# Retention's deviations taken on all partitions in the next phase, branch A's weights two chunks ahead, denser filling

## The chip, the cores and the metric

The kernel runs on one core of a Trainium2 chip. The metric is the device time of one execution in microseconds (us). The core's engines run side by side, each through its own queue in order: TensorE (PE) multiplies, VectorE (DVE), ScalarE (ACT) and GpSimd (POOL) work on elements, SyncE (SP) mostly issues DMAs. A wait at the head of a queue holds all that stands behind it there.

## The reference

One layer over 2048 tokens of width 1024, all in fp32 (cut):

```python
h = rms_norm(x, norm_gain[l])
proj = jnp.einsum('bsd,df->bsf', h, w_in[l])
q_a, k_a, v_a, g_a, q_r, k_r, v_r, g_r, m_a, m_r = split_columns(proj)
o_a = chunk_band_attention(q_a, k_a, v_a, rel_bias[l])           # 8 heads, chunks of 64, 8 chunks to the left
branch_a = jnp.einsum('bsf,fd->bsd', o_a * jax.nn.silu(g_a), w_out_attn[l])
o_r = retention_chunkwise(rotary(q_r), rotary(k_r), v_r, gn_gain[l])   # ends in:
#   o = (o - mean) * lax.rsqrt(var + GN_EPS), mean and var over the 128 values of a head
branch_r = jnp.einsum('bsf,fd->bsd', o_r * jax.nn.silu(g_r), w_out_ret[l])
mixed = jax.nn.sigmoid(m_a) * branch_a + jax.nn.sigmoid(m_r) * branch_r
x = rms_norm(x + jnp.einsum('bsd,de->bse', mixed, w_out[l]), final_gain)
```

## The kernel before

The tokens are worked in two halves of 1024, and each fp32 operand is split into a high and a low part (`wh`, `wl` for weights, the two tiles of `R[m]` for activations), so that a product of a 128x128 weight block takes three matmuls of 512 columns instead of one.

All dense products form one **stream**, made by `dense` (line 451): jobs p0 and g0 (projections and gates of the first half), p1 and g1 (second half), ba0 and ba1 (output product of branch A, the attention), br0 and br1 (branch B, the retention), out. A projection chunk is a Strassen scheme of seven products, gathered in PSUM banks x, y, v, z, w; a chunk of ba0 or ba1 is four plain products. A product is 12 matmuls, handed out in four **steps** of three. The counts are p0 up to step 392, g0 784, p1 1176, g1 1568, ba0 1632, ba1 1696, br1 1952, out 2208.

The phases are `proj0`, attention and retention of half 0, `proj1`, attention and retention of half 1, and `mrg`, the rest. Inside attention and retention, `fill(n)` lets the stream go on by n steps between the small matmuls of the phase, so that the other engines get time; `RET_FILLS` (line 60) is the number of steps that retention gives away twice per item (32 items per half: a pair of heads, a block of 256 tokens, one head of the pair). `later(n, fn)` (line 242) puts a piece of work off by n steps; `put` does so with a store. Up to the end of the second retention every engine gets its instructions in the order in which the code issues them; in `mrg` a scheduler may reorder ACT, DVE and POOL, while PE and SP stay in order.

`prime` (line 440) prepares the weights three products ahead: ACT casts `wh`, and DVE (or POOL) makes `wl` four steps later. The raw weights lie in a ring of three buffers (`RAWS`). In the stream, a chunk of a plain job is loaded over SP at the first product of the chunk ahead of it (line 474), so four products before its own start for ba0 and ba1.

In `retention` (line 1371) each item makes scores `sr` (PE), masks them with `dm` into `sm` (DVE), splits them into `sh` (ACT) and `sl` (POOL), and multiplies by the values into `o`; `oz` and `o` are copied and squared out of PSUM (ACT), `o2l` is the low part of the squares (POOL). Squares are summed over a head by matmuls with one-hot weights into the PSUM tile `ssq`, 32 rows (head and block) by 512 tokens. After the last item a chain of twelve DVE instructions on 32x512 tiles (`rt`, lines 1600 to 1615) makes the reciprocal roots, one instruction per step, and stores them to `rsscr`.

`finish_yr` (line 1071) reads them back as `rb`, spread over 128 partitions, and finishes one head and block of branch B (`yr` on DVE, then on POOL). While g0's last chunk runs, `reload` (line 799) puts the 28 activation tiles of half 1 into `R` (loads `r<-cs` on SP, ACT cast, DVE or POOL `r<-r`). In the second half `refill` does the same with `oas` (attention) and `yrs` (branch B).

Every instruction issued through the helper of line 140 carries that line in the profile, so rows are told apart by their tiles: `ps_g_z` is bank z of a gates job, `c_g` and `u_g` are the sums taken from such banks, `t_p` the Strassen sums of weights, `raw_ba` a raw chunk of branch A.

## Time and profile before

| | us |
|---|---|
| runs of the kernel before | 1987.76 median of 3 (1986.89 to 1991.05) |
| the profiled execution | 1993.2 |
| its span, first to last instruction | 1991.4 |
| PE busy in the span | 1926.9 |
| DVE busy | 1353.9 |
| ACT busy | 911.1 |
| POOL busy | 898.8 |

The profile is of one execution, in which the span plus 1.8 us around it makes its time. Its views name each instruction by engine, line, operation and tiles, and give an engine's idle time before it with what ended that. "PEclk" is the TensorE clock that was granted, as a share of full speed. A matmul's end is modelled, so what a wait costs PE is seen best from start to start.

### The profile page before, as it was taken

Reading aid. Unit: us, or ns where it says so; the run is one execution under the profiler, and the core shown is the slowest. Engines: PE = TensorE matmul, PEld = TensorE weight load, DVE = VectorE, ACT = ScalarE, POOL = GpSimd, SP = SyncE. Lnnn points to the kernel's source line nnn. Section 1 sums busy time; section 2 is a strip of 40 time slices with the busy share of each in tenths; the row PEclk is TensorE's granted clock in tenths of the full one; section 3 lists DMA queues with packets and bytes.
Section 4 is the critical chain, followed back from the end, with each engine's and each line's share of the span. In section 5 each row is a group of like instructions: output and inputs, shape, how many; then the busy total and the mean of one; then the engine's idle time right before and its main releaser. Section 6 shows DMA issues by size and latency. Waiting matters only on the chain.

```text
span 1991.4 us, 30303 instructions
## 1 busy us (share of the span) xinstructions
PE 1926.9 (97%) x9712; PEld 1604.3 (81%) x9712; DVE 1353.9 (68%) x2585; ACT 911.1 (46%) x1835; POOL 898.8 (45%) x735
## 2 busy tenths in 40 slices
PE   6899999999999999999999999999999999999998
PEld 4777778888888877778787888888888878888886
DVE  7887878677766658888887677765566655544554
ACT  6454454566654545443333555554455221222332
POOL 2343544555546665544544444454675114422222
PEclk9999999999999999999999999999999999999999
DMA  4576695756549987676675645554989999976564
GB/s 148 162 258 198 217 309 197 211 153 181 159 135 276 276 248 258 192 242 195 193 247 177 185 148 177 155 147 141 281 268 294 319 334 338 326 251 213 187 200 138
DMA packets 335054, 434.85 MB, mean 218 GB/s; under 512 B 30040, under 2 KB 194544, under 8 KB 334896
## 3 DMA queue, kind: packets, MB, share of 16 engines
q1 hardware_dynamic: 277744, 377.07, 59.6%
q10 hardware_dynamic: 57152, 55.85, 9.3%
q8 instruction: 78, 1.28, 0.3%
q14 instruction: 80, 0.66, 0.1%
HBM read 288.21 MB, written 144.60 MB: 217 GB/s over the span
## 4 chain that ended last, share of the span: by engine, by line
PE 50%; DVE 7%; DMA 4%; issue 3%; ACT 1%; POOL 1%; SPq 0%; DVEq 0%; POOLq 0%; ACTq 0%
PE ps_g_z L140 4%; PE ps_g_x L140 3%; PE ps_p_z L140 3%; PE po L140 2%; PE ps_p_x L140 2%; PE wide L140 2%; PE o L140 2%; PE ps_g_v L140 2%; PE ps_g_y L140 2%; PE ps_g_w L140 2%; PE tp L140 1%; PE ps_p_w L140 1%; PE ps_p_y L140 1%; DMA raw_ba<-in_w_out_attn_dram 1%; PE ps_p_v L140 1%
## 5 line engine op out<-in xcount | busy, mean ns | idle before, releaser
L140 POOL TENSOR_SCALAR pr<-pr,rsum 128x640 f32<-128x640 f32 (+4 forms) x128 | 96.5, 754 | 225.4 <-DVE ptl L140 105.4
L140 PE MATMUL ps_g_z<-r,wh_g 128*128 128x512 f32 x448 | 144.0, 403 | 4.2 <-DVE c_g L140 4.2
L140 PE MATMUL ps_p_z<-r,wh_p 128*128 128x512 f32 x448 | 141.5, 397 | 5.4 <-DVE c_p L140 2.8
L140 PE MATMUL ps_p_x<-r,wh_p 128*128 128x512 f32 x448 | 142.0, 398 | 1.4 <-ACT u_p L140 1.4
L140 PE MATMUL ps_g_x<-r,wh_g 128*128 128x512 f32 x448 | 142.5, 399 | 0.7 <-ACT u_g L140 0.7
L140 DVE CUSTOM_DVE_ANT_0 pr<-wide,bt 128x640 f32<-128x640 f32 (+4 forms) x128 | 94.3, 737 | 71.2 <-PE wide L140 63.8
L140 POOL TENSOR_TENSOR t_p<-raw_p,t_p 128x512 f32<-128x512 f32 x50 | 74.8, 1497 | 146.9 <-DVE wl_p L140 134.1
L140 ACT ACTIVATE pr<-pr,mn 128x640 f32<-128x640 f32 (+4 forms) x128 | 98.0, 766 | 85.0 <-DVE mn L140 85.0
L140 DVE TENSOR_TENSOR ptl<-tp,pth 128x384 fp32r<-128x384 f32 x168 | 95.9, 573 | 40.9 <-ACT pth L140 40.5
L140 ACT CAST pth<-tp 128x384 fp32r<-128x384 f32 x168 | 84.8, 516 | 70.1 <-PE tp L140 66.1
L140 POOL TENSOR_TENSOR sl<-sm,sh 128x512 fp32r<-128x512 f32 x64 | 88.0, 1376 | 61.5 <-ACT sh L140 25.5
L140 DVE TENSOR_TENSOR wl_p<-t_p,wh_p 128x512 fp32r<-128x512 f32 x112 | 105.1, 939 | 2.0 <-ACT wh_p L140 2.0
L1167 POOL TENSOR_TENSOR fg<-xr,fg 128x512 f32<-128x512 f32 x32 | 44.4, 1387 | 128.3 <-DVE xr L1161 100.5
L140 DVE TENSOR_TENSOR sm<-sr,dm 128x512 f32<-128x512 f32 x64 | 44.1, 689 | 82.7 <-DMA dm<-in_dmask_dram 35.2
L140 PEld LDWEIGHTS ps_p_z<-r,wh_p 128*128 128x128 f32 x448 | 81.7, 188 | 22.9 <-issue 5.5
L140 PEld LDWEIGHTS ps_p_x<-r,wh_p 128*128 128x128 f32 x448 | 83.7, 190 | 19.9 <-ACT u_p L140 2.2
L140 PE MATMUL wide<-ka,qa 128*128 128x512 f32 (+2 forms) x448 | 94.5, 327 | 2.3 <-DVE mn L140 2.3
L1125 POOL TENSOR_TENSOR gr<-gr,ta 128x512 f32<-128x512 f32 x32 | 47.7, 1492 | 105.0 <-DVE gr L1124 89.8
L140 POOL TENSOR_TENSOR wl_g<-t_g,wh_g 128x512 fp32r<-128x512 f32 x56 | 75.2, 1342 | 40.5 <-ACT wh_g L140 31.4
L140 PEld LDWEIGHTS tp<-ident,pr 128*128 128x128 f32 x560 | 71.2, 140 | 27.2 <-POOL pr L140 2.2
L140 PE MATMUL po<-pth,va 128*128 128x256 f32 x336 | 93.0, 297 | 0.0
L140 ACT CAST wh_p<-t_p 128x512 fp32r<-128x512 f32 x112 | 69.2, 619 | 49.5 <-PE ps_p_z L140 22.1
(1187 smaller groups left out, 5969.2 us busy)
## 6 DMA issues: line engine op xcount, KB each, us to landing
raw_g<-in_w_in_dram ACTq DMA_DIRECT2D x56, 512.0 KB, 5.4
raw_p<-in_w_in_dram ACTq DMA_DIRECT2D x50, 512.0 KB, 6.1
qa<-qas SPq DMA_DIRECT2D x128, 128.0 KB, 3.0
qr<-qrs SPq DMA_DIRECT2D x128, 128.0 KB, 4.2
vr<-vrs SPq DMA_DIRECT2D x64, 256.0 KB, 5.6
ka<-kas SPq DMA_DIRECT2D x40, 256.0 KB, 3.6
va<-vas SPq DMA_DIRECT2D x40, 256.0 KB, 3.0
kds<-kdt_k SPq DMA_DIRECT2D x32, 256.0 KB, 4.5
```

What stands on the lines that cost most here:

```text
L140: return tc.keep_in_program_order(op(*a, **k))
L1125: pool.tensor_tensor(g, g, ta, ALU.add)
L1167: pool.tensor_tensor(fg, xr, fg, ALU.mult)
```

## The change

Three things, in the code:

- `RET_FILLS` goes from (1.9, 2.2) to (2.0, 2.3).
- At the end of `retention` one ACT instruction scales `ssq` into `var` and a store takes it to a new scratch, `sqscr`. The chain runs in a new function, `deviations`, which loads those numbers as 128 partitions by 128 columns, adds the epsilon, takes the roots in twelve DVE instructions of 128x128 (one per step) and stores them to `rsscr`. It is called 6 steps into the projection of half 1 for half 0 and 24 steps into `mrg` for half 1. The eight `finish_yr` of half 0 start at 38 and come every 42 steps, where they started at 10 and came every 44.
- `dense` loads a chunk of ba0 and ba1 seven products before its own start instead of four.

In steps: retention of half 0 ended at 772 and now ends at 769, that of half 1 at 1600 and now at 1597; the last item ends at step 757 instead of 750, and at 1585 instead of 1578.

```diff
-RET_FILLS = (1.9, 2.2)
+RET_FILLS = (2.0, 2.3)
...
+    sqscr = [D(f"sqs_{s}", [32, B]) for s in range(2)]
...
+    def firsts_of(seq):
+
+        seen = set()
+        for at, (_, ch, _n) in enumerate(seq):
+            if ch not in seen:
+                seen.add(ch)
+                yield at, ch
...
+        short = {begins_plain - 7: ch for begins_plain, ch in firsts_of(seq) if ch.job.kh == 1}
...
+            if at in short and short[at].raw is None:
+                short[at].load()
...
-        y, tmp, hv, var = (E(f"rt{n}")[0:32] for n in range(4))
+        var = E("var")[0:32]
+        later(1, lambda: act.activation(var, ssq, AF.Copy, scale=1.0 / DV))
+        put(3, sqscr[s], var)
+        fill(3)
+
+    def deviations(s):
+
+        t = E(f"dev_{s}", shape=(P, 4, P))
+        v, y, tmp = (t[:, n] for n in range(3))
+        wide_ = lambda d: d.rearrange("r (q c) -> (r q) c", c=P)
+        dma(v, wide_(sqscr[s]))
         chain = [
-            lambda: dve.tensor_scalar(var, ssq, 1.0 / DV, GN_EPS, ALU.mult, ALU.add),
-            lambda: dve.tensor_scalar(tmp.bitcast(I32), var.bitcast(I32), 1, None, ALU.logical_shift_right),
+            lambda: dve.tensor_scalar(v, v, GN_EPS, None, ALU.add),
+            lambda: dve.tensor_scalar(tmp.bitcast(I32), v.bitcast(I32), 1, None, ALU.logical_shift_right),
...
-                lambda: dve.scalar_tensor_tensor(tmp, y, -0.5, var, ALU.mult, ALU.mult),
+                lambda: dve.scalar_tensor_tensor(tmp, y, -0.5, v, ALU.mult, ALU.mult),
...
-        chain.append(lambda: dma(rsscr[s], y))
         for n, fn in enumerate(chain):
-            later(1 + n, fn)
-        fill(len(chain))
+            later(9 + n, fn)
+        later(9 + len(chain) + 2, lambda: dma(wide_(rsscr[s]), y))
...
+    later(6, lambda: deviations(0))
     for h in range(HEADS):
-        later(10 + 44 * h, lambda h=h: finish_yr(h, 0, None, 18))
+        later(38 + 42 * h, lambda h=h: finish_yr(h, 0, None, 18))
...
+    later(24, lambda: deviations(1))
```

DVE at the end of the first retention, **before** (`rt` is the chain; `wl`, `u2`, `c22` belong to the gates' chunks 12 and 13, `r01` is a refilled activation tile):

```order
L140 TENSOR_TENSOR wl_g0_13_1_8977<-t2_g0_13_8809,wh_g0_13_1_8976 128x512
L140 TENSOR_SCALAR rt3_9015<-ssq_6950 32x512
L140 TENSOR_SCALAR rt1_9013<-rt3_9015 32x512
L140 TENSOR_SCALAR rt0_9012<-rt1_9013 32x512
L140 SCALAR_TENSOR_TENSOR rt1_9013<-rt0_9012,rt3_9015 32x512
L140 TENSOR_TENSOR rt1_9013<-rt1_9013,rt0_9012 32x512
L140 SCALAR_TENSOR_TENSOR rt0_9012<-rt1_9013,rt0_9012 32x512
L140 TENSOR_TENSOR wl_g0_13_4_9032<-t1_g0_13_8807,wh_g0_13_4_9031 128x512
```

and **now**, from the same `wl` on:

```order
L140 TENSOR_TENSOR wl_g0_13_1_8956<-t2_g0_13_8745,wh_g0_13_1_8955 128x512
L140 TENSOR_TENSOR wl_g0_13_4_9024<-t1_g0_13_8743,wh_g0_13_4_9023 128x512
L140 TENSOR_TENSOR u2_g0_13_9014<-ps_g0_13_y_9053,u2_g0_13_9014 128x512
L140 TENSOR_TENSOR r01_82<-r01_82,r00_81 128x512
L140 TENSOR_TENSOR u3_g0_13_9117<-ps_g0_13_v_9085,u2_g0_13_9014 128x512
L140 TENSOR_TENSOR r01_82<-r01_82,r00_81 128x512
L140 TENSOR_TENSOR wl_g0_13_6_9081<-raw_g0_13_1_8551,wh_g0_13_6_9080 128x512
L140 TENSOR_TENSOR c22_g0_13_9144<-ps_g0_13_z_9129,u3_g0_13_9117 128x512
```

All twelve instructions of the chain are gone from there, also the six that stood between the second `wl` and `c22`.

DVE early in the projection of half 1, **before** (`l_qa`, `l_ka` are low parts of queries and keys, `wl_p1` low weights of its first two chunks, `r31`, `r51` refilled tiles):

```order
L140 SCALAR_TENSOR_TENSOR l_qa_2_0_9269<-ps_p1_0_x_9227,h_qa_2_0_9268 128x512
L140 TENSOR_TENSOR r51_92<-r51_92,r50_91 128x512 x2
L140 TENSOR_TENSOR wl_p1_1_1_9275<-t2_p1_1_9225,wh_p1_1_1_9274 128x512
L140 TENSOR_TENSOR r51_92<-r51_92,r50_91 128x512
L140 TENSOR_TENSOR wl_p1_0_2_9307<-t3_p1_0_9251,wh_p1_0_2_9306 128x512
L140 TENSOR_TENSOR l_ka_2_0_9326<-ps_p1_1_x_9279,h_ka_2_0_9325 128x512
L140 TENSOR_TENSOR r31_88<-r31_88,r30_87 128x512
```

and **now**:

```order
L140 SCALAR_TENSOR_TENSOR l_qa_2_0_9259<-ps_p1_0_x_9215,h_qa_2_0_9258 128x512
L140 TENSOR_TENSOR r51_92<-r51_92,r50_91 128x512 x2
L140 TENSOR_TENSOR wl_p1_1_1_9265<-t2_p1_1_9213,wh_p1_1_1_9264 128x512
L140 TENSOR_SCALAR dev_0_9244<-dev_0_9244 128x128 x2
L140 TENSOR_TENSOR r51_92<-r51_92,r50_91 128x512
L140 TENSOR_SCALAR dev_0_9244<-dev_0_9244 128x128
L140 TENSOR_TENSOR wl_p1_0_2_9291<-t3_p1_0_9239,wh_p1_0_2_9290 128x512
L140 SCALAR_TENSOR_TENSOR dev_0_9244<-dev_0_9244 128x128
L140 TENSOR_TENSOR l_ka_2_0_9312<-ps_p1_1_x_9269,h_ka_2_0_9311 128x512
L140 TENSOR_TENSOR r31_88<-r31_88,r30_87 128x512
L140 TENSOR_TENSOR dev_0_9244<-dev_0_9244 128x128
L140 SCALAR_TENSOR_TENSOR dev_0_9244<-dev_0_9244 128x128
```

The chain, now `dev`, is spread one by one between the refills and the low weights; its other six instructions follow before `u3` of the first chunk, and the `yr` instruction that stood there has moved later.

SP in branch A's second job, **before** (`tas` stores and `ga` loads go with one product each, `yr`, `yv`, `rb` belong to `finish_yr`):

```order
L140 DMA tas_5_1_419<-ga_5_1_18043 128x512
L140 DMA ga_7_0_18122<-mas_7_0_362 128x512
...
L140 DMA rb_3_1_18185<-rss_0_439 128x512
L140 DMA tas_7_0_426<-ga_7_0_18122 128x512
L140 DMA raw_ba1_1_0_18195<-in_w_out_attn_dram 128x4x256
L140 DMA ga_0_3_18197<-mas_0_3_337 128x512
```

and **now**:

```order
L140 DMA tas_5_1_419<-ga_5_1_18042 128x512
L140 DMA dev_1_18115<-sqs_1_440 128x128
L140 DMA raw_ba1_1_0_18117<-in_w_out_attn_dram 128x4x256
L140 DMA ga_7_0_18122<-mas_7_0_362 128x512
L140 DMA tas_6_0_422<-ga_6_0_18064 128x512
```

The load of a raw chunk stands three `tas` stores, that is three products, earlier. In the tail of the second retention the same move puts `raw_ba0_1`, which stood behind the last values `vr_3_7`, directly ahead of `kd_3_6` and `vr_3_6`. At the end of the first retention the store of the roots (`rss`), which stood ahead of the weight loads of p1's second chunk and of the last 16 `r<-cs` loads, gives way to the store of `var` four loads further forward.

## Rows read from the trace of the kernel before

**Rows 1.** The page's busy time, share of the span and instructions of each engine.

```profile
PE 1926.9 (97%) x9712; PEld 1604.3 (81%) x9712; DVE 1353.9 (68%) x2585; ACT 911.1 (46%) x1835; POOL 898.8 (45%) x735
```

**Rows 2.** Windows: stretch, length; busy PE, PEld, DVE, ACT, POOL (count); PEclk; DMA share, GB/s.

```profile
573.00:762.00 189.00, 181.75 (x1030) 155.62 (x1029) 111.41 (x198) 92.43 (x175) 113.35 (x87) 0.99 0.78 236
1395.00:1557.00 162.00, 160.17 (x929) 139.47 (x929) 99.44 (x168) 86.58 (x160) 94.79 (x71) 1.00 0.92 284
1557.00:1640.00 83.00, 80.77 (x348) 64.41 (x347) 52.87 (x84) 20.65 (x36) 10.31 (x8) 1.00 0.94 327
...
774.00:784.00 10.00, 8.09 (x31) 6.24 (x30) 9.17 (x16) 4.33 (x8) 2.82 (x1) 0.85 0.63 189
784.00:800.00 16.00, 14.65 (x62) 11.46 (x61) 16.00 (x16) 11.10 (x22) 11.88 (x9) 0.99 1.04 380
```

**Rows 3.** PE's waits in 573 to 762 us: who waited for whom, us, times, longest.

```profile
PE ps_g_z L140 <- DVE c_g L140: 2.3, 1, 2.3
PE o L140 <- ACT o L140: 1.7, 3, 0.9
```

**Rows 4.** Groups of the chain on DVE, 760 to 780 us: busy us, mean ns.

```profile
L140 DVE SCALAR_TENSOR_TENSOR rt<-rt,rt 32x512 f32<-32x512 f32 x6 | 7.1, 1189 | 0.1
L140 DVE TENSOR_TENSOR rt<-rt,rt 32x512 f32<-32x512 f32 x3 | 3.0, 1007 | 0.1
L140 DVE TENSOR_SCALAR rt<-rt 32x512 int32<-32x512 int32 x2 | 1.8, 906 | 0.1
L140 DVE TENSOR_SCALAR rt<-ssq 32x512 f32<-32x512 f32 x1 | 0.7, 678 | 1.2 <-PE ssq L140 1.2
```

**Rows 5.** Timelines of DVE, then PE, after the chain: start, us, what, [idle before].

```profile
778.74 0.67 DVE L140 TENSOR_TENSOR c_g<-ps_g_z,u_g 128x512 f32<-128x512 f32 x1
...
779.56 0.70 PE L140 MATMUL ps_g_z<-r,wh_g 128*128 128x512 f32 x2 [1.91 <-DVE c_g L140]
```

**Rows 6.** Timeline of SP at the same place: start, us, DMA issued.

```profile
776.43 0.33 SPq L140 DMA_DIRECT2D rss<-rt  x1
...
779.54 7.32 SPq L140 DMA_DIRECT2D r<-cs  x12
```

**Rows 7.** Groups of all DVE work: the one that is nearest to 128x128.

```profile
L140 DVE SCALAR_TENSOR_TENSOR state<-state,kv 64x128 f32<-64x128 f32 x48 | 11.4, 274 | 16.8 <-PE kv L140 14.7 <-DMA mas<-g 2.1
```

**Rows 8.** Timelines of POOL, DVE and PE (in this order) early in proj1.

```profile
801.09 1.74 POOL L140 TENSOR_TENSOR t_p<-raw_p,t_p 128x512 f32<-128x512 f32 x1
...
807.54 1.30 POOL L140 TENSOR_TENSOR yr<-yr,rb 128x512 f32<-128x512 f32 x1 [1.29 <-DVE yr L140]
...
801.60 1.78 DVE L140 TENSOR_TENSOR r<-r,r 128x512 fp32r<-128x512 f32 x1
803.30 0.68 DVE L140 TENSOR_TENSOR u_p<-ps_p_y,u_p 128x512 f32<-128x512 f32 x1
...
806.72 0.74 DVE L140 SCALAR_TENSOR_TENSOR yr<-yr,gn,yv 128x512 f32<-128x512 f32 x1
...
814.53 0.50 PE L140 MATMUL ps_p_w<-r,wl_p 128*128 128x512 f32 x1 [0.38 <-DVE wl_p L140]
818.53 0.50 PE L140 MATMUL ps_p_w<-r,wl_p 128*128 128x512 f32 x1 [0.96 <-DVE wl_p L140]
```

**Rows 9.** Branch A: PE's first and last wait of three, SP's load, `raw_ba`'s landing times.

```profile
1599.36 0.74 PE L140 MATMUL ps_ba_(0, 0)_18298<-r,wh_ba_(0, 0)_18218 128*128 128x512 f32 x2 [1.01 <-ACT wh_ba_(0, 0)_18218 L296]
...
1623.73 0.73 PE L140 MATMUL ps_ba_(0, 0)_18490<-r,wh_ba_(0, 0)_18414 128*128 128x512 f32 x2 [0.57 <-ACT wh_ba_(0, 0)_18414 L296]
...
1591.32 0.39 SPq L140 DMA_DIRECT2D raw_ba<-in_w_out_attn_dram  x1
...
DMA to landing us min/median/max: 3.9/5.4/7.3
```

**Rows 10.** Second retention: one of PE's waits, 1395 to 1557 us; a window.

```profile
PE kv L140 <- DMA vr<-vrs: 0.7, 2, 0.5
...
1520.00:1530.00 10.00, 10.00 (x60) 8.78 (x60) 8.18 (x15) 7.38 (x14) 5.41 (x4) 1.00 1.03 337
```

## The prediction

> **What bounds the kernel now.** I read the shares of busy time first: PE is busy for 1926.9 us, 97% of the span, the other engines for 68% at most [rows 1]. The matmuls are the same in number and size after the change, so it can gain only where PE stands still or runs at the lower clock. The views to read are therefore the table of windows, for what PE lacks in each stage, and then the waits and timelines inside the stages that the change touches.
>
> Between 573 and 762 us (retention of half 0) PE is busy 181.75 of 189.00 us, so it idles 7.2 us; its mean granted clock of 0.99 costs another 1% of 189, 1.9 us. Between 1395 and 1557 us (most of the second retention) it idles 1.8 us at full clock [rows 2]. The two stages do the same work, but the first gives 1.9 steps to the stream at each place and the second 2.2. What PE waits for in the first is spread: `c_g`, a sum on DVE, once for 2.3 us, and `o`, which ACT has to copy out of PSUM, 1.7 us in three waits [rows 3].
>
> Right behind the first retention, between 774 and 784 us, PE idles 1.9 us and the granted clock is 0.85 [rows 2]. The timelines name the cause: product 6 of the last gates chunk waits 1.91 us for `c_g`, which DVE starts at 778.74 [rows 5], just behind the chain of roots. That chain takes DVE 7.1 + 3.0 + 1.8 + 0.7 = 12.6 us [rows 4]. SP stood in the same place: it issues the store of the roots at 776.43 and gets to the next twelve loads of `r<-cs` from 779.54 on [rows 6].
>
> In branch A, between 1557 and 1640 us, PE idles 83.00 - 80.77 = 2.2 us [rows 2], in three waits, each for the cast of a raw chunk (1.01 us the first, 0.57 the last). SP issued the first of those chunks at 1591.32 for a product that began at 1599.36, and such a load takes 3.9 to 7.3 us to land [rows 9].
>
> **The change part by part.** One step of the stream is 3 matmuls. In branch A 348 matmuls take 80.77 us [rows 2], 0.232 us each, so a step is 0.70 us and a product (12 matmuls) 2.8 us.
>
> *The chain leaves the end of the first retention.* DVE gets 12.6 us back there, and in its order nothing of the chain is left ahead of `c_g`. The bank's product 4 then has the whole of product 5, 2.8 us, as cover for a sum of 0.67 us [rows 5]. So I take the wait as gone: 1.9 us, and the lower clock behind it: (1 - 0.85) x 10 + (1 - 0.99) x 16 = 1.7 us [rows 2]. Together **-3.6 us**; no less than 0 and, with the waits named next also gone, 1.3 us more. ACT takes one instruction more, nothing to speak of at 911.1 us of 1991 [rows 1]. SP no longer stands until 776.43, so the refills of half 1 come earlier, which hides in the same gain.
>
> *The chain comes back in the projection of half 1.* By the order it stands among refills and low weights, from step 799 to 810, which in the trace of before is 795 to 805 us. There DVE has no time to spare: it is busy for all 16.00 us from 784 to 800 [rows 2], and soon after PE waits for `wl_p`, 0.38 and 0.96 us [rows 8]. The nearest row for one new instruction is 0.274 us, 64 partitions by 128 columns [rows 7]; twelve make 3.3 us. Against that `yr` of `finish_yr` leaves the stretch: 0.74 us on DVE, and 1.30 us of POOL [rows 8] of which DVE may wait most. Net 3.3 - 0.74 - 1.1 = 1.5 us of DVE time. Half of the chain comes before 800 us, where DVE is now ahead instead of behind, so I take half: **+0.7 us**. The lower bound is 0, the upper one follows from the next sentences.
>
> A `r<-r` (two operands in SBUF) takes 1.78 us when it starts inside a POOL instruction that runs from 801.09 for 1.74 us, and `u_p`, with one operand in PSUM, 0.68 us [rows 8]; the chain itself shows it too, with means of 1.19 and 1.01 us for instructions of which the first, from PSUM, took 0.68 [rows 4]. So a new instruction on SBUF may cost 1.78 - 0.68 = 1.1 us more whenever it meets POOL, however few columns it has: 12 x 1.1 + 1.5 = 14.7 us is the upper bound. The Trainium skill, in SBUF — State Buffer, section "SBUF: two separate sides", states this as a rule: VectorE and GpSimd share a port pair under an exclusive lock, held "for the full instruction". By that rule cutting 512 columns to 128 saves nothing of the wait, and the trace agrees as far as the 1.78 us shows. It speaks against this change and is the third rival below.
>
> I stay near the lower end because POOL runs no more instructions there than before, and nearly all of them hold a DVE instruction already; more DVE instructions don't make more POOL instructions to wait for.
>
> *The new DMAs.* The load of `dev` is issued 9 steps, 6.3 us, ahead of the chain; landing takes 3.9 to 7.3 us for far larger loads [rows 9], so it is hidden. The store stands on SP two steps behind the chain, and behind it wait stores of queries and keys and the loads of `finish_yr`, which nobody needs for tens of steps: 0, at worst 1 us. The roots are first needed at step 822.
>
> *The second chain.* It leaves the tail of the second retention and returns in branch A. From 1557 on PE waits for nothing but raw chunks, and DVE is busy 52.87 of 83.00 us, POOL 10.31 [rows 2]. Nothing on either side: 0.
>
> *Denser filling.* The steps are only moved, so each 0.1 buys slack alone: 0.1 x 0.70 us between any two small products. If the first retention at 1.9 lacks 7.2 + 1.9 = 9.1 us and the second at 2.2 lacks 1.8, the slope is 2.4 us for each 0.1. I take **-2.4 us** for the first. It may get all that the second has (-7.3); and since the stream's chunks slide against retention's items, a wait like the longest may fall in anew: 2.3 us and the 1.7 us of lower clock, +4.0. For the second I take 0 (bounds -1.8 and +1).
>
> *Branch A's weights.* Three products earlier is 8.4 us earlier; the three loads were late by 1 us at most [rows 9]. All 2.2 us go, and the slow first matmuls behind each wait (0.74 us for two, against 2 x 0.232) with them, about 0.16 x 3: **-2.7 us**, bounds -3 and 0. What becomes late next is nothing that waits today: three waits are all that the stretch has. But the second chunk of branch A now goes out directly ahead of the values of two of retention's last items, where the transfers run at 337 GB/s with a DMA share of 1.03 and PE already waits 0.7 us for `vr` [rows 10]. 512 KB at that rate are 1.6 us of delay, and denser filling gives back some: **+0.7 us**, bounds 0 and 1.6.
>
> The sum: -3.6 + 0.7 - 2.4 - 2.7 + 0.7 = **-7.3 us**. The profiled execution took 1993.2 us, span and surroundings, so it would take 1985.9. It lies 5.4 us over the median of its kernel's runs, 1987.76; the difference carried over gives **1980.5 us**.
>
> **The rivals.**
>
> *The waits of retention only slide.* The first retention gets no better but a wait like its longest more: +4.0 instead of -2.4, so -7.3 + 6.4 = -0.9 us, 1986.9: no change. For it: the waits have several causes [rows 3], and the stream is moved by only 7 steps in 140. Against it: the second retention, with more filling, has almost none.
>
> *Branch A's loads don't land earlier.* SP keeps order, and transfers are busy for 0.94 of the time [rows 2]. Then 2.7 us are missing: 1983.1. Against it: the order puts the load three `tas` stores forward, each of which waits for a product.
>
> *The chain meets POOL (slower).* In the projection of half 1, from 795 to 805 us, every one of the twelve waits for a POOL instruction, DVE falls 14.7 us behind, and PE waits for `wl_p` that long: -7.3 - 0.7 + 14.7 = +6.7 us, 1994.5. It decides from the point where 1.5 + 1.1 x n is over 8.0, that is from 6 of the 12 on. Against it: a POOL instruction takes 1.74 us there [rows 8], so ten us hold six at the most, and those already hold others. The skill's SBUF page, named above, would have this come out by its lock.
>
> *Everything clears.* The first retention does as the second (-7.3 in place of -2.4), and the `wl_p` waits go because DVE enters the projection without arrears (-1.3 and the +0.7): -7.3 - 4.9 - 2.0 = -14.2, 1973.6.
>
> **How the numbers follow.** The forecast has 0.55, the sliding waits 0.20, the late loads 0.08, POOL 0.07, everything clear 0.10. 0.2% of 1987.76 is 4.0 us, about what a measurement of this kernel can tell from no change: faster means below 1983.8. The forecast's spread of some 4 us either way puts 0.50 of its 0.55 there; with 0.05 of the late loads, 0.10 of the clear case and 0.02 of the sliding one that is 0.67. Slower is 0.06 from POOL and 0.01 from sliding waits, 0.07. The rest, 0.26, is no change. The range goes from 1973 to 1988: it holds the sliding case and the edge of the clear one, and leaves out POOL's.
>
> **What would show it.** Right: no wait for `c_g` behind the first retention and a clock of 1.00 there; no wait for `wh_ba`; PE's idle time in the first retention at some 5 us; waits for `wl_p` early in the projection no longer than 2 us. Wrong: `dev` rows of over 1 us each; a wait for `vr` of over 2 us at the end of the second retention; new waits of over 2 us with a clock near 0.5 in the first.

## The result, and the profile after

| | median of runs | runs |
|---|---|---|
| before, in the same session | 1987.11 us | 21 |
| changed kernel | 1992.53 us | 21 |
| ratio, changed to before | 1.0027, 95% interval 1.0019 to 1.0035 | |
| changed kernel again, in a later session (e12) | 1989.32 us against 1986.87; 1.0020, 1.0004 to 1.0036 | 11 and 27 |

By the two ratios the change costs 4 to 5 us; the medians differ by 5.4 and 2.5 us. The forecast was 1980.5, so it is 12 us too low and has the wrong sign. A few executions in the experiments were slow ones of over 2100 us, which the ratios leave out and the medians do not (e6's stands 0.8 us higher for it), so the readings go by the ratios.

The profiled execution of the changed kernel took 1999.27 us, 6.7 over its median. PE's line of the page, which answers to [rows 1]:

```profile
PE 1928.5 (97%) x9712; PEld 1608.2 (81%) x9712; DVE 1337.6 (67%) x2585; ACT 909.5 (46%) x1837; POOL 890.1 (45%) x735
```

The windows of the changed kernel that answer to [rows 2] (stretch, length; busy PE, PEld, DVE, ACT, POOL with counts; PE's granted clock; DMA share, GB/s):

```profile
573.00:762.00 189.00, 185.23 (x1062) 159.79 (x1061) 111.41 (x201) 95.62 (x182) 118.13 (x91) 1.00 0.82 247
...
774.00:784.00 10.00, 8.61 (x37) 6.43 (x37) 10.00 (x9) 7.31 (x14) 8.14 (x6) 1.00 1.05 394
...
1395.00:1557.00 162.00, 156.19 (x892) 134.92 (x891) 94.55 (x159) 81.39 (x153) 89.84 (x68) 0.99 0.89 274
1557.00:1640.00 83.00, 80.45 (x354) 66.09 (x353) 49.42 (x83) 22.44 (x40) 11.89 (x9) 0.98 0.96 332
```

PE's idle time in the first retention fell from 7.2 to 3.8 us, and the wait for `c_g` behind it is gone, as forecast. But the second retention, which idled 1.8 us, now idles 5.8, and branch A idles 2.5 us against 2.2. Both kernels were profiled once more, the kernel before as e11 and the changed kernel as e12, and much of this doesn't repeat. The kernel before, unchanged, idles 3.7 us in the same window of its second profile:

```profile
573.00:762.00 189.00, 185.32 (x1059) 159.16 (x1057) 117.79 (x206) 95.88 (x182) 118.16 (x90) 1.00 0.82 246
```

So the 3.8 us are no gain that can be put down to the change. In the other two windows e11 idles 2.4 and 1.4 us, e12 3.8 and 0.2.

In both profiles of the changed kernel PE no longer waits for a raw chunk in branch A [rows 9]. In the first one it waits for an epilogue on DVE, `ga`, instead; in e12 that wait is 0.2 us. The waits of PE from 1557 to 1640 us in the first profile (who for whom, us, times, longest), and DVE's timeline there (start, us, what, idle time before it and its releaser):

```profile
PE ps_ba_(1, 1)_18383 L140 <- DVE ga L1119: 2.6, 1, 2.6
```

```profile
1608.94 0.75 DVE L1092 SCALAR_TENSOR_TENSOR yr<-yr,gn,yv 128x512 f32<-128x512 f32 x1 [0.96 <-DMA yv<-urs]
1611.74 0.69 DVE L1102 TENSOR_TENSOR r<-yr,r 128x512 fp32r<-128x512 f32 x1 [2.05 <-ACT r L1101]
...
1613.55 0.68 DVE L1119 SCALAR_TENSOR_TENSOR ga<-ga,ps_ba_(1, 1)_18280 128x512 f32<-128x512 f32 x1
```

DVE takes its instructions in order. It stands 0.96 us for a load of `finish_yr` and 2.05 us for ACT's copy in the same helper, and the `ga` that would free PE's bank is queued behind both.

The larger losses lie in the projection of half 1, where the forecast had +0.7 us. The chain there, by groups on DVE from 784 to 803 us (busy us, mean ns), in the place of [rows 4]:

```profile
L140 DVE SCALAR_TENSOR_TENSOR dev<-dev 128x128 f32<-128x128 f32 x6 | 4.2, 693 | 0.1
L140 DVE TENSOR_TENSOR dev<-dev 128x128 f32<-128x128 f32 x3 | 3.0, 996 | 0.0
L140 DVE TENSOR_SCALAR dev<-dev 128x128 int32<-128x128 int32 x2 | 0.4, 224 | 0.0
L140 DVE TENSOR_SCALAR dev<-dev 128x128 f32<-128x128 f32 x1 | 0.2, 217 | 0.0
```

These are 7.8 us, against 12 x 0.274 = 3.3 us by [rows 7]. The timelines of DVE, POOL and PE at this place show why (`dev` rows of DVE, the POOL rows that run beside them, PE's next wait):

```profile
790.23 1.38 DVE L140 TENSOR_TENSOR dev<-dev 128x128 f32<-128x128 f32 x1
791.64 1.27 DVE L140 SCALAR_TENSOR_TENSOR dev<-dev 128x128 f32<-128x128 f32 x1
...
794.74 0.28 DVE L140 TENSOR_TENSOR dev<-dev 128x128 f32<-128x128 f32 x1
...
798.74 1.33 DVE L140 TENSOR_TENSOR dev<-dev 128x128 f32<-128x128 f32 x1
800.00 1.75 DVE L140 TENSOR_TENSOR wl_p<-t_p,wh_p 128x512 fp32r<-128x512 f32 x1
...
789.72 1.74 POOL L140 TENSOR_TENSOR t_p<-raw_p,t_p 128x512 f32<-128x512 f32 x1
791.42 1.34 POOL L140 TENSOR_TENSOR t_p<-b_p,t_p 128x512 f32<-128x512 f32 x1
792.72 1.34 POOL L140 TENSOR_TENSOR r<-r,r 128x512 fp32r<-128x512 f32 x1
795.52 1.45 POOL L140 TENSOR_TENSOR r<-r,r 128x512 fp32r<-128x512 f32 x1 [1.46 <-ACT r L140]
...
798.34 1.58 POOL L140 TENSOR_TENSOR t_p<-raw_p,t_p 128x512 f32<-128x512 f32 x1
...
801.80 0.55 PE L140 MATMUL ps_p_z<-r,wl_p 128*128 128x512 f32 x1 [3.92 <-DVE wl_p L140]
```

The `dev` of 790.23 starts inside POOL's `t_p`, which runs to 791.46, and ends at 791.61. The one of 791.64 ends at 792.91, behind a POOL instruction that runs to 792.76; the one of 798.74 at 800.07, behind one to 799.92. Each ends 0.15 us after POOL. The one of 794.74 falls in POOL's gap (794.06 to 795.52) and takes 0.28. Five of the twelve were held; the two that are not shown took 0.78 and 1.27 us and also ended 0.15 us after POOL. One that started 0.02 us behind a POOL instruction, at 795.54, was not held (0.28 us). `wl_p` comes behind them, and PE waits 3.92 us for it; in the kernel before it waited 0.38 and 0.96 us for other `wl_p`, two and six microseconds further into the stage [rows 8].

The second chain, in branch A, has the same twelve instructions with the same operands in SBUF, and no POOL instruction but one of 0.02 us runs beside it: there each takes 0.22 to 0.29 us, in both profiles. So it is the place that makes the chain slow, not the instructions.

Later in the same projection PE waits 1.78 us for `u_p`, a wait that the trace of before doesn't have. DVE, then POOL, then PE, in the changed kernel:

```profile
851.87 0.74 DVE L140 SCALAR_TENSOR_TENSOR yr<-yr,gn,yv 128x512 f32<-128x512 f32 x1
852.53 1.78 DVE L140 TENSOR_TENSOR xk<-xk,t_k 128x512 f32<-128x512 f32 x1
854.23 1.78 DVE L140 TENSOR_TENSOR u_p<-u_p,cs_k 128x512 f32<-128x512 f32 x1
856.05 1.63 DVE L140 TENSOR_TENSOR u_p<-u_p,t_k 128x512 f32<-128x512 f32 x1
...
852.03 1.73 POOL L140 TENSOR_TENSOR t_p<-raw_p,raw_p 128x512 f32<-128x512 f32 x1 [2.43 <-DVE wl_p L140]
853.72 1.74 POOL L140 TENSOR_TENSOR yr<-yr,rb 128x512 f32<-128x512 f32 x1
...
857.74 0.33 PE L140 MATMUL trkr_k<-ident,u_p 128*128 128x128 f32 x1 [1.78 <-DVE u_p L140]
```

The same two instructions on DVE in the kernel before:

```profile
858.89 0.68 DVE L140 TENSOR_TENSOR xk<-xk,t_k 128x512 f32<-128x512 f32 x1
859.50 1.78 DVE L140 TENSOR_TENSOR u_p<-u_p,cs_k 128x512 f32<-128x512 f32 x1
```

`u_p` is as slow there as in the changed kernel; what is new stands ahead of it. `yr` of the later `finish_yr` takes 0.66 us from start to start, and `xk`, which started 0.16 us before POOL's `t_p` (859.05) and took 0.68, now starts 0.50 us behind it and takes 1.78. That is 0.66 + 1.10 = 1.76 us, the wait of PE, whose transposes of `xk` and `u_p` come next. The POOL half of the same `yr` then runs beside `u_p`, where the kernel before has another POOL instruction.

The same stages in all profiles, from the first small product of a retention or the first product of a projection to the next such mark, read from PE's timelines. "First 14" and "rest" are the projection of half 1 up to the start of its fourteenth product after the first, and from there to its last; "ret 1 to B" goes from the second retention's first product to branch B's.

| kernel | ret 0 | first 14 | rest | ret 1 to B |
|---|---|---|---|---|
| before | 184.8 | 42.9 | 248.4 | 247.6 |
| before, again (e11) | 176.8 | 43.1 | 248.3 | 248.4 |
| changed | 173.8 | 46.3 | 253.6 | 254.8 |
| changed, again (e12) | 172.2 | 47.2 | 251.2 | 246.9 |
| e1: filling 2.0, 2.2 | 176.1 | 45.5 | 248.3 | 248.0 |
| e2: filling 1.9, 2.3 | 176.9 | 43.0 | 248.4 | 252.2 |
| e3: early loads | 179.7 | 43.1 | 248.3 | 244.6 |
| e4: `finish_yr` later | 184.0 | 41.0 | 252.6 | 249.1 |
| e5: chain and `finish_yr` | 178.7 | 47.1 | 252.6 | 249.9 |
| e6: changed, filling 2.0, 2.2 | 175.0 | 47.1 | 251.1 | 244.4 |
| e7: changed, no early loads | 173.0 | 46.4 | 253.8 | 248.9 |
| e8: changed, `y` in PSUM | 171.5 | 42.8 | 252.4 | 247.0 |
| e9: e8, `finish_yr` at 54 + 44h | 178.0 | 42.8 | 248.4 | 248.3 |
| e10: e9, filling 2.0, 2.2 | 173.3 | 42.8 | 248.3 | 247.5 |
| e13: filling 1.9, 2.3, early loads | 181.5 | 43.1 | 248.4 | 248.8 |
| e14: filling 2.0, 2.2, early loads | 176.7 | 45.2 | 248.3 | 249.9 |
| e15: chain as in e9, alone | 179.2 | 42.8 | 248.3 | 250.9 |

### The profile page after: what moved, and what is told of

Read it like the earlier page. It is cut to its first block, busy times and chain, and to the rows that moved or that the text cites. A ratio compares the mean times of both kernels' runs of the same rounds, so it can differ in the third digit from the quotient of the medians.

```text
span 1997.5 us, 30305 instructions
## 1 busy us (share of the span) xinstructions
PE 1928.5 (97%) x9712; PEld 1608.2 (81%) x9712; DVE 1337.6 (67%) x2585; ACT 909.5 (46%) x1837; POOL 890.1 (45%) x735
## 5 line engine op out<-in xcount | busy, mean ns | idle before, releaser
L140 DVE TENSOR_TENSOR wl_p<-t_p,wh_p 128x512 fp32r<-128x512 f32 x112 | 100.2, 896 | 1.9 <-ACT wh_p L140 1.9
L140 PE MATMUL ps_p_z<-r,wl_p 128*128 128x512 f32 x224 | 89.9, 401 | 4.0 <-DVE wl_p L140 3.9
L140 PE MATMUL tp<-ident,pr 128*128 128x128 f32 x560 | 88.9, 272 | 2.9 <-POOL pr L140 1.6
```

What stands on the lines that cost most here:

```text
L140: return tc.keep_in_program_order(op(*a, **k))
```

## The experiments

Each is given with its median, that of before on the same chip, and the ratio with its 95% interval, from 8 to 11 executions (5 in e2 and e7). The ratio isn't the quotient of the two medians and differs from it by up to 0.0006 here.

### The chain and `finish_yr` by themselves

**e5** is the changed kernel without the early loads and with the old fillings:

```diff
-RET_FILLS = (2.0, 2.3)
+RET_FILLS = (1.9, 2.2)
...
-            if at in short and short[at].raw is None:
-                short[at].load()
```

> The changed kernel with the old filling (1.9, 2.2) and the old loads of branch A: only the chain of roots is moved, with finish_yr at its new times. Theory A (each part acts in its own stage): the wait for c_g behind the first retention and its lower clock are gone, 3 to 4 us; the twelve instructions early in the projection cost 3 to 4 us, through waits for wl_p, and the later yr 4 to 6 us; branch A and the second retention are as before: 3 to 6 us slower. Theory B (the parts lose only together): within 2 us of before or faster.

1997.97 against 1987.92 us, 1.0048 (1.0029 to 1.0066). This part alone makes the kernel slower, by some 9.5 us, more than the 3 to 6 of theory A. The waits of PE from 776 to 816 us in e5 show the same long one as the changed kernel:

```profile
PE ps_p_z L140 <- DVE wl_p L140: 4.0, 1, 4.0
```

**e4** is the kernel before with `finish_yr` at its later place, the chain left where it was:

```diff
-        later(10 + 44 * h, lambda h=h: finish_yr(h, 0, None, 18))
+        later(38 + 42 * h, lambda h=h: finish_yr(h, 0, None, 18))
```

> The kernel before with the eight finish_yr of half 0 at 38 + 42 h steps instead of 10 + 44 h, the chain of roots unchanged. Theory A (the 5 us that the changed kernel lost from 826 us to the end of half 1's projection come from yr meeting the rotations, whose two-operand instructions wait for POOL): that stretch is 4 to 6 us longer, with waits for u_p near 856 and 984 us of 1.8 and 0.8 us; the stretch before it is 1 to 2 us shorter, as yr leaves it. Theory B (they are arrears of the new chain): the stretch is unchanged within 1 us.

1990.73 against 1987.92, 1.0015 (1.0000 to 1.0029). The table shows it: -2.0 us in the first fourteen products (41.0 against 43.0, the gain from `yr` leaving them), +4.3 in the rest. That is theory A. In its DVE timeline `xk` is slow behind `yr` as in the changed kernel, without any chain:

```profile
856.54 0.74 DVE L140 SCALAR_TENSOR_TENSOR yr<-yr,gn,yv 128x512 f32<-128x512 f32 x1
857.21 1.78 DVE L140 TENSOR_TENSOR xk<-xk,t_k 128x512 f32<-128x512 f32 x1
```

**e8** is the changed kernel with one tile of the chain, `y`, in PSUM. Ten of the twelve instructions then have an operand there (nine of them, the number in the expectation, read it):

```diff
-        v, y, tmp = (t[:, n] for n in range(3))
+        v, last, tmp = (t[:, n] for n in range(3))
+        y = TR(f"devy_{s}")[:, 0:P]
...
-                lambda: dve.scalar_tensor_tensor(y, tmp, 1.5, y, ALU.add, ALU.mult),
+                lambda k=k: dve.scalar_tensor_tensor(last if k == 2 else y, tmp, 1.5, y, ALU.add, ALU.mult),
```

> The changed kernel with one tile of the chain, y, kept in PSUM; only its last result goes to SBUF. Of the twelve instructions nine then have an operand in PSUM. Theory A (an instruction of the chain with both operands in SBUF stands until the POOL instruction beside it ends): the dev rows that took 1.3 to 1.6 us in the changed kernel fall to 0.3 to 0.5, DVE is back some 4 us earlier, the wait for wl_p of 3.9 us in the early projection of half 1 falls to about 1, and the stretch from its first product to the fourteenth after it gets 3 to 5 us shorter; the time falls by 2 to 5 us. Theory B (the wait for wl_p comes from DVE being late with refills and low weights whatever the chain costs, or from the transfers): rows shorter, wait and stretch as in the changed kernel within 1.5 us, the time within 2 us.

1986.82 against 1989.44, 0.9993 (0.9980 to 1.0006); the changed kernel stands at 1.0027 and 1.0020, 5 to 7 us higher. Groups of the chain on DVE in e8, and in its timelines a `dev` that starts inside a POOL instruction (787.52, with POOL's `t_p` from 785.89 for 1.75 us):

```profile
L140 DVE SCALAR_TENSOR_TENSOR dev<-devy,dev 128x128 f32<-128x128 f32 x3 | 0.9, 285 | 0.0
L140 DVE TENSOR_TENSOR dev<-dev,devy 128x128 f32<-128x128 f32 x3 | 0.8, 274 | 0.0
L140 DVE SCALAR_TENSOR_TENSOR devy<-dev,devy 128x128 f32<-128x128 f32 x2 | 0.6, 288 | 0.0
...
787.52 0.28 DVE L140 SCALAR_TENSOR_TENSOR dev<-devy,dev 128x128 f32<-128x128 f32 x1
...
785.89 1.75 POOL L140 TENSOR_TENSOR t_p<-raw_p,t_p 128x512 f32<-128x512 f32 x1
```

No instruction of the chain takes over 0.3 us, the sum is the 3.3 us that [rows 7] gave, and the first fourteen products take 42.8 us where the kernels with the chain in SBUF take 46.3 to 47.2. So theory A holds: 3.9 us of the stage (46.7, the mean of the four kernels with the chain in SBUF and the filling 2.0, less 42.8) is the chain's standing beside POOL. Of PE's wait 1.6 us is left. The `wl_p` that PE waits for ends 28.62 us after the stage's first product in the changed kernel (801.75 - 773.13) and 25.87 in e8, so DVE's delay is 2.8 of the 3.5 us between these two profiles. The mean granted clock of the stage is 0.96 and 0.93 in the two profiles of the changed kernel, 1.00 in e8: behind its wait PE runs at the lower of its two levels for a while (0.50 from 803 to 805 us in the first). What the time fell beyond the 3.9 us lies within the intervals of the ratios.

**e9** is e8 with `finish_yr` at steps 54 + 44h:

```diff
-        later(38 + 42 * h, lambda h=h: finish_yr(h, 0, None, 18))
+        later(54 + 44 * h, lambda h=h: finish_yr(h, 0, None, 18))
```

> The kernel with y in PSUM, and finish_yr at steps 54 + 44h instead of 38 + 42h: the spacing of before and, modulo 44, its place among the products, one head later. Theory A (the 4 us that every kernel with the later finish_yr loses in the rest of the projection, from the fourteenth product to the last, 252.4 to 253.8 us against 248.3, come from the new place of yr just ahead of u_p on DVE): the stretch falls back to 248 to 249 us, no wait for u_p of over 0.9 us, the time 3 to 5 us under that of the kernel with y in PSUM, so about 1982 to 1984. Theory B (they come from yr being moved behind the chain at all, wherever it then falls): the stretch stays at 252 or more, the time at about 1987.

1982.78 against 1986.87, **0.9976 (0.9963 to 0.9989)**: faster than both kernels. The waits of PE from 819 us to the end of the projection, first in the changed kernel (820 to 1073), then in e9 (820 to 1072):

```profile
PE trkr_k L140 <- DVE u_p L140: 2.6, 2, 1.8
PE ps_p_z L140 <- DVE c_p L140: 2.3, 2, 1.2
PE trva L140 <- DVE c_p L140: 2.2, 2, 1.1
```

```profile
PE trva L140 <- DVE c_p L140: 2.8, 2, 1.6
PE ps_p_z L140 <- DVE c_p L140: 1.2, 2, 0.8
PE ps_p_y L140 <- DVE wl_p L140: 0.4, 1, 0.4
```

No wait for `u_p`, and the stage is back at 248.4 us: theory A. It was the place of `yr` among the products, not its being later. The seven kernels with `yr` at the bad place have the same waits in this stage, 7.1 us in the sum against 4.2 in the kernel before. That difference, 2.9 us, is about what e6 and e12 lose, at a mean granted clock of 1.00; the other five have 0.99 and lose 4 to 5.5 us.

### The fillings

**e1**, `RET_FILLS = (2.0, 2.2)` in the kernel before:

> The kernel before with RET_FILLS (2.0, 2.2) alone; the chain of roots stays at the end of each retention. Theory A (the first retention's own filling made most of the 11 us that the changed kernel gained up to the first product of half 1's projection): the stretch from the first score of the first retention to that product is 6 to 8 us shorter than before, the wait for c_g behind the chain (1.9 us) stays, and the whole is some 7 us faster. Theory B (the gain came from taking the chain away): that stretch is at most 3 us shorter, the whole within 3 us of before.

1988.13 against 1987.92, 1.0006 (0.9994 to 1.0017): nothing, as in theory B. The stretch of 176.1 us can't tell between the theories, as the kernel before takes 184.8 in one profile and 176.8 in the other. The waits of PE in e1 from 760 to 790 us:

```profile
PE ps_p_x L140 <- ACT u_p L140: 3.4, 2, 2.8
PE ps_g_z L140 <- DVE c_g L140: 2.6, 1, 2.6
```

With the chain still at the end of the first retention, the wait for `c_g` grows from 1.9 [rows 5] to 2.6 us and one for `u_p` of 2.8 us comes behind it; the first fourteen products take 45.5 instead of 43.0.

**e2**, `RET_FILLS = (1.9, 2.3)` in the kernel before:

> The kernel before with RET_FILLS (1.9, 2.3) alone. Theory A (the second retention lost its 5 us to the filling of 2.3, which shifts the stream's chunks against the items): PE idles 5 to 8 us from 1385 to 1540 us, with a wait of some 2 us for ACT's copy of o, and the whole is 4 to 6 us slower. Theory B (it lost them to branch A's loads, which now go out ahead of the values): PE's idle time there stays at 1.8 us, the whole is within 2 us of before.

1998.37 against 1987.92, 1.0058 (1.0038 to 1.0078). The time is past both theories, and neither names the place: from 1385 to 1540 us PE idles 1.5 us, with no wait for `o` on ACT. It loses in branch A (`ga`, 2.0 and 1.6 us, and the casts of raw chunks) and in branch B (one wait of 2.0 us for ACT's copy `r`). **e13** adds the early loads to it:

> The kernel before with the second retention filled at 2.3 and branch A's weights loaded earlier: the pair that was not yet run together without the chain. Theory A (2.3 is dear only because branch A then comes earlier against its weights and its gates, and the early loads pay for that): no wait for wh_ba, the stage from the second retention to branch B 246 to 250 us instead of 252, and the time within 3 us of before, 1984 to 1990. Theory B (2.3 is dear by itself): 1994 to 1998, as the kernel with 2.3 alone.

1994.93 against 1987.88, 1.0039 (1.0025 to 1.0052): by the time theory B. The loads don't pay for 2.3, though the wait for `wh_ba` is gone and the stage is at 248.8 us; part of the loss lies behind it. From branch B's first product to the last instruction the kernel takes 359.7 us here and 360.6 in e2, and 356.4 to 357.2 in all other profiles. PE's waits in e13 from 1570 to 1740 us, and what DVE waits for from 1570 to 1610:

```profile
PE ps_ba_(1, 1)_18369 L140 <- DVE ga L1118: 2.4, 1, 2.4
PE ps_br_(0, 1)_19372 L140 <- ACT r L1100: 2.0, 1, 2.0
PE ps_ba_(1, 1)_18171 L140 <- DVE ga L1118: 1.9, 1, 1.9
```

```profile
DVE r L1101 <- ACT r L1100: 6.0, 4, 2.2
DVE yr L1091 <- DMA yv<-urs: 3.8, 4, 1.3
DVE ga L1118 <- DMA ga<-mas: 2.4, 3, 1.4
```

It is the same queue as in the first profile of the changed kernel: `finish_yr` on DVE waits for loads and for ACT, and `ga` stands behind. A denser filling takes the stream further before branch A's phase opens, so `finish_yr` and the loads of the gates come later against the products that use them. That last step is argued from the order, not shown.

**e6**, the changed kernel with the filling (2.0, 2.2):

> The changed kernel with the second retention filled at 2.2 as before, all else as changed. Theory A (the filling of 2.3 alone costs the second retention and branch B some 5 to 10 us, as in the kernel with that edit alone): 5 to 10 us faster than the changed kernel, so about 1982 to 1987, with the stage from the second retention's first product to branch B at 248 to 250 us instead of 254.8. Theory B (in the changed kernel the slower second retention comes from the later finish_yr work and from the chain's late store that slide against it): the stage stays near 254 us and the time near 1992.

1990.13 against 1989.44, 1.0008 (0.9991 to 1.0024). Between the theories: 2 to 4 us under the changed kernel, less than theory A's 5, with intervals that overlap, and with the stage at 244.4. **e10** is e9 with (2.0, 2.2):

> The kernel with y in PSUM and finish_yr at 54 + 44h, and the second retention filled at 2.2 as before. Theory A (2.3 costs the second retention something: the changed kernel took 2.4 us more than its twin at 2.2): 2 to 4 us under its sibling with 2.3, about 1979 to 1981. Theory B (the long second retention of the profile of the changed kernel was one draw from a spread, and 2.3 costs nothing): within 1.5 us of its sibling, and the stage from the second retention's first product to branch B at 244 to 248 us in both.

1982.95 against 1986.87, 0.9982 (0.9971 to 0.9993), the same as e9 within the intervals: theory B. Where the chain has left the second retention's end, 2.3 costs nothing that e9 and e10 can tell; where it stays (e2, e13), 2.3 costs 8 to 11 us. That the chain makes the difference, with the 13 steps of filling that it brings there, is argued: no run changes it alone at 2.3.

### The early loads

**e3**, the kernel before with the early loads of branch A alone:

> The kernel before with branch A's weights loaded earlier and nothing else of the change. The singles so far stand at +0.2 us (filling of the first retention), +10.5 (filling of the second), +2.8 (finish_yr later) and +10.1 (chain with finish_yr later), the whole change at +5.4. Theory A, the parts add: 0.2 + 10.5 + 10.1 = 20.8, so the loads would have to give back some 15 us, and this kernel runs about 1973. Theory B, the parts overlap (a stall in one stage is taken by the slack of the next): the loads take away the three waits for raw chunks in branch A, about 2 us, at most 4: 1984 to 1987. Both expect no wait for wh_ba in branch A.

1988.06 against 1989.44, 0.9999 (0.9984 to 1.0014). The stage is shorter, 244.6 us, but the time is not; a wait for `ga` of 1.0 us came in place of the raw chunks. Theory A, that parts add up, falls; the 1984 to 1987 of theory B aren't reached either.

**e7**, the changed kernel without them:

> The changed kernel without the early loads of branch A's weights. Theory A, the parts add: 1988 + 20.8 = about 2008, 15 us above the changed kernel. Theory B, the parts overlap: the three waits for raw chunks in branch A come back, 2 to 3 us, so about 1995; or 1992 as the changed kernel, if the wait for ga on DVE, 2.55 us in branch A of the changed kernel, ends last there anyway.

1995.94 against 1989.44, 1.0034 (1.0020 to 1.0047), against the changed kernel's 1.0027 and 1.0020. Here the loads are worth 1 to 3 us, between e2 and e13 some 4, in e3 nothing, and each of these differences is within the intervals.

### One profile is a draw

**e11** and **e12** are the kernel before and the changed kernel once more, with a second profile of each:

> The kernel before, once more, for a second profile. Theory A (the first retention took 184.8 us in the first profile because this kernel's filling of 1.9 starves it): 183 to 186 us from its first product to the projection again. Theory B (that stage is a draw: kernels with the same code up to its end took 176.9 to 184.0): it can be anywhere from 176 to 185, most likely near their middle, 180, and nothing is to be read from one profile of it.

> The changed kernel, once more, for a second profile. Its first profile is of an execution of 1999.3 us, 6.7 us over its median. Theory A (the second retention and branch A are slow in it because of the filling of 2.3): 253 to 256 us again from the second retention's first product to branch B. Theory B (a draw): 245 to 250 us as in the kernel with y in PSUM, which has the same code there. Both: the wait for wl_p of 3.9 us in the early projection and the 1.8 us for u_p later come again, since every kernel with these parts has them.

Windows over the first retention and over the rest of the projection, first of the first profile of before, then of the second:

```profile
598.71:783.53 184.82, 175.79 (x980) 149.87 (x979) 119.72 (x199) 91.78 (x173) 112.90 (x84) 0.98 0.83 254
...
826.39:1074.74 248.35, 243.96 (x1124) 199.94 (x1123) 202.74 (x276) 93.03 (x178) 111.28 (x75) 1.00 0.69 219
```

```profile
599.68:776.43 176.75, 171.95 (x980) 147.72 (x979) 119.17 (x199) 90.87 (x171) 111.71 (x84) 1.00 0.87 265
...
819.50:1067.84 248.34, 243.96 (x1125) 199.96 (x1123) 203.25 (x276) 92.91 (x178) 111.26 (x75) 1.00 0.69 219
```

The same 980 matmuls take 8 us less, while the projection repeats to 0.01 us. Six profiles with the same code up to there (before, e11, e2, e3, e4, e13) give the first retention 176.8 to 184.8 us. In the second profile the wait for `c_g` behind it is again 1.9 us, but the mean granted clock of the 10 us around it is 1.00, not 0.85 (in the first profile about three of the ten were granted 0.50, the lower level). So theory B of e11 holds. The second retention of the changed kernel is such a draw too: 254.8 us in one profile, 246.9 in the other, while the waits for `wl_p` (3.9 us) and `u_p` (1.8 us) come again, as theory B of e12 has it.

**e15** and **e14** ask what the chain's move is worth when it meets neither POOL nor `u_p`. e15 is the kernel before with the chain of e9 and nothing else; e14 has the filling (2.0, 2.2) and the early loads, and the chain in its old place:

> The chain moved with y in PSUM and finish_yr at 54 + 44h, and nothing else of the change: fillings 1.9 and 2.2, no early loads. Theory A (the term of the prediction for the chain's leaving, -3.6 us, is right in kind, and only what the moved work met at its new place was wrong): 2 to 4 us under before, 1983 to 1985, with no wait for c_g behind the first retention and 42.8 us for the first fourteen products of the projection. Theory B (the c_g wait is paid anyway, or its slack is taken by the next stage): within 1 us of before.

> The kernel before with the first retention filled at 2.0 and branch A's weights loaded earlier; the chain of roots stays where it was. It tells whether moving the chain is worth anything beside these two. Theory A (the chain at the end of the first retention eats what 2.0 gives: with 2.0 alone PE waited 2.6 us for c_g and 2.8 for u_p there): 1985 to 1988, 2 to 5 us over the kernel that has the chain moved with y in PSUM, finish_yr at 54 + 44h and the same fillings (1983). Theory B (the move of the chain gives nothing even when done so): 1981 to 1984.

e15: 1986.58 against 1987.88, 0.9993 (0.9982 to 1.0005). e14: 1987.04 against 1987.88, 1.0001 (0.9989 to 1.0014). The chain's leaving gives 1.4 us by itself, with an interval that holds zero, and less than theory A of e15 has. Together with 2.0 it seems to give more: e10, which is e14 with the chain moved as in e9, stands at 0.9982, 3.8 us below (0.0019 x 1988). That fits theory A of e14, that the denser filling pays only once the chain isn't in its way; but the two intervals overlap (0.9971 to 0.9993, 0.9989 to 1.0014), so it is indicated and not shown.

## Why the prediction was wrong, by its own steps

| step | forecast | measured | from |
|---|---|---|---|
| chain leaves the first retention | -3.6 | -1.7 at 1.9, -2.6 at 2.0, neither clear of the spread | e5, e15 against the six; seven chainless at 2.0 against e1, e14 |
| filling of the first retention | -2.4 | -4 to -5 in the stage; with the chain there, +2.3 behind it and 0 in the time | e1, e14, e5, e15 |
| chain in the early projection | +0.7 | +3.7, of which the wait for POOL is 3.9 | changed, e5 to e8 |
| `finish_yr` later: rest of the projection | not costed | +4.1, of which 2.9 are waits | e4, e9 |
| filling of the second retention | 0 | -1 to +4 with the chain gone, +8 to +11 with it | e9 against e10, changed against e6; e2, e13 |
| early loads, with their price | -2.0 | 0 to -4 | e3, e7, e2 against e13 |

The measured column takes stage lengths from the table, as means over the kernels with the same code in the stage: 180.6 us for the first retention in the six, 178.9 in e5 and e15, 176.4 in e1 and e14, 173.8 in the seven others, with a spread of 6 to 8 us among kernels with the same code; 43.0 against 46.7 for the first fourteen products; 248.3 against 252.5 for the rest.

**The step left out.** The prediction moved `finish_yr` and counted only what it leaves: 0.74 us of DVE and 1.30 of POOL. At its new place it costs 4.1 us, twice the 2.0 that its leaving gives (e4). The trace of before shows `xk` and `u_p` on DVE just ahead of the transposes that take them, with `xk` only 0.16 us ahead of a POOL instruction; the prediction did not look at the new place.

**The step that was mis-sized.** The prediction named the rival and its rule, and weighed it down with: "POOL runs no more instructions there than before, and nearly all of them hold a DVE instruction already; more DVE instructions don't make more POOL instructions to wait for". That sentence is true in part only. Five of twelve were held, which is 7.8 - 3.3 = 4.5 us of DVE time; DVE came 2.8 us later to the `wl_p` that PE needs, so by this count other instructions would have taken some 1.7 us of the holding, and 2.8 is new: POOL instructions that else meet instructions with an operand in PSUM and hold none of them, as most of the `t_p` of 785.89 in e8. The stage lost 3.9 by it. Without that (e8) it takes 42.8 against 43.0, so the rest of the sum (3.3 us of chain against what `yr` leaves) was about right, at -0.2. By the rival's own count (from six held instructions on) the chain decides the sign; five held, with the place of `yr`, were enough. The rival's twelve were too many in any case: nine of the twelve read two tensors, and the three `TENSOR_SCALAR` read one and ran while POOL was idle, so no run shows whether they can be held. The rule in the Trainium skill, SBUF — State Buffer, section "SBUF: two separate sides", that a VectorE instruction with two inputs in SBUF and a GpSimd instruction that reads SBUF shut each other out for a whole instruction, is borne out twice: by the `dev` rows that end 0.15 us behind POOL's (with the one exception at 795.54), and by e8, in which one operand in PSUM takes the wait away. The words that the prediction quotes from that page stand there under "Terms".

**The reading of one profile.** The term for the chain's leaving had 1.7 us for the lower clock behind the `c_g` wait; the second profile of before has the wait without it. The slope of 2.4 us per 0.1 of filling came from a first retention that had drawn 184.8 us; from e11 the same working gives none: 3.7 us of idle time at a clock of 1.00 in the first window, against 2.4 us and 1.6 for a clock of 0.99 in the second. The sum for the stage, -6.0, is close to the mean over profiles (173.8 - 180.6 = -6.8), but that is luck: neither part gives anything clear of noise in the time alone (e1, e15). One figure of the early loads is also wrong as worked: 0.74 less 2 x 0.232 is 0.28, not 0.16.

**What was right.** No wait for `c_g` behind the retention, the wait for `wh_ba` gone, `dev` loaded in time (its first row has no wait before it), the second chain free of cost on DVE (3.3 us, none of it held). The idle time of 3.8 us in the first retention, where some 5 were forecast, proves nothing, as e11 has 3.7 without the change. Among the signs for being wrong the prediction had `dev` rows of over 1 us, and four came. The late wait for `vr` was not what came next in branch A: in the first profile the `ga` epilogue on DVE was, and that the prediction did not see, because it read DVE's 52.87 of 83 us [rows 2] as room, where what counts is what stands ahead of `ga` in the queue.

**What stays open.** From the second retention to branch B the two profiles of the changed kernel take 250.9 us in the mean, the six at 2.2 without early loads 249.0. The stages then sum to -6.8 + 3.7 + 4.1 + 1.9 = +2.9 us, and the times say +4 to +5. Seven and six profiles with a spread of 6 to 8 us in the first retention don't settle the difference. Nor is it shown why `ret 1 to B` differs by 8 us between two profiles of the changed kernel: half of it is PE's idle time (8.7 against 4.8 us), half its busy time (246.1 against 242.1 us, at mean granted clocks of 0.99 and 1.00), but the code is the same.

## What to carry to other kernels

Work that is moved has a cost at its new place as well as a gain at the old one, and each of the things that move with it needs its own look at the neighbours there, by name, in the trace: here a helper of two instructions cost more than it gave. Making the chain's instructions on VectorE smaller did not shorten those that met GpSimd; an operand in PSUM did. A stage whose length differs between executions of the same code should be read from several profiles before a slope is taken from it, and a wait that goes can let in the next one, here one on another engine.

## What the runs showed of the hardware

A 128x128 instruction on VectorE with two inputs in SBUF takes 0.28 us; where it was held by GpSimd it took 0.78 to 1.38 us, ending 0.15 us after the GpSimd instruction each time. With one of the inputs in PSUM it took 0.27 to 0.30 us in the same stretch (e8). The first retention, with a DMA share of 0.83 to 0.87, varied by 8 us between executions of the same code; the later part of the projection, with 0.69, repeated to 0.14 us in seven profiles of the same code. That the transfers make the difference is not shown: with the later `finish_yr` that same part took 253.6 and 251.2 us in two executions of one kernel, at a DMA share of 0.67. And the same PE wait of 1.9 us stood once beside a mean granted clock of 0.85 over 10 us and once beside 1.00.
